# Adaptive-norm gates spread by a DMA, retention split from PSUM, decay moved behind the projection

## The chip, the cores and the metric

The kernel runs on one core of a Trainium2 chip. The metric is the device time of one execution in microseconds (us); a smaller number is better. A core has five engines with instruction streams of their own: TensorE (PE in the profile, weight loads under PEld), VectorE (DVE), ScalarE (ACT), GpSimd (POOL) and SyncE (SP), which here only issues DMA transfers. Each stream is worked off in order; the engines wait for each other through semaphores.

## What is computed

The program is a two-layer encoder on 256 tokens of width 1024. One layer of the reference, cut:

```python
cond = jax.nn.silu(c)
mod = (cond @ w_ada[i] + b_ada[i])[:, None, :]
sh1, sc1, g1, sh2, sc2, g2 = jnp.split(mod, 6, axis=-1)
h = _rmsnorm(x, norm1_g[i]) * (1.0 + sc1) + sh1
q_a, k_a, v_a, u_s, q_r, k_r, v_r, g_r = jnp.split(h @ w_in[i], split_at, axis=-1)
...                      # attention y_a, S5 scan y_s, retention y_r (each from its columns)
mixed = jnp.concatenate([y_a, y_s, y_r], axis=-1) @ w_out[i]
x = x + g1 * mixed
h = _rmsnorm(x, norm2_g[i]) * (1.0 + sc2) + sh2
x = x + g2 * _hier_moe(h, ...)
# retention, per head: scores (rotated q, k) times a decay gamma^(i-j), times v;
# then each head is normalised, scaled by gn_g and gated by silu(g_r)
```

The adaptive-norm rows of one layer are 6144 numbers. The two gates g1 and g2 multiply whole rows, so the kernel needs them repeated on all 128 partitions. The shifts and scales are needed as columns.

## The kernel before

The token axis is two blocks of 128 (t). Each layer has a mixing stage, then an expert stage.

In the mixing stage the weights of the projections come in 1 MB pieces on SP's queue. Each piece is split into a high part by ScalarE (L685) and a low part by VectorE (L686), and three products of the parts make one exact product on TensorE: `product`, whose matmuls are L710 (tokens on the partitions) and L705 (turned). The input projection runs five blocks of columns: block 0 is retention's q and k, block 1 its v and gate, blocks 2 to 4 the attention's. At the end of a block a function evicts the bank from PSUM: L845 (`to_qkr`, on VectorE, times the decay), L841, L849 and L852 (copies on ScalarE). TensorE's order is written by hand: `at(g, f)` puts a piece of other work between the steps of the projection. That is the S5 scan (matmuls L463 and L497; VectorE's products L473 to L476, the scan L480, and L483 and L484 behind it, whose result L497 needs), retention (`rope`, `turn`, `scores`, `mix`, `out`) and the remaining adaptive-norm products. The order of the other engines follows from a scheduler with priorities, in which the weight splits stand high.

The adaptive norm (`ada_slot`) has three groups of 2048 numbers per layer. The first is done ahead of the stage; groups 1 and 2 are sixteen steps within the projection, each four matmuls (L204) that leave the same row on 32 partitions. After eight steps `ada_row` copies the sum out of PSUM on ScalarE (L228), and `ada_finish` transposes it on TensorE (L234) and adds the bias on VectorE (L235), so that `modT` holds columns. `gate_row` (L243) makes a row on all partitions out of such columns: four matmuls of a repeated column with the identity (L250) and an eviction on ScalarE (L251), twice for 1024 columns. It is called for g1 among the fillers of the output projection (`fill`, between the attention's L579) and for g2 in the route of the expert stage (`filler`), ahead of the next layer's first adaptive-norm group (L204).

In retention `scores` multiplies the two diagonal blocks by a mask on VectorE (L630) and copies the third on ScalarE (L632); `mix` copies the output out of PSUM on ScalarE (L643) and normalises it on VectorE (L645 to L659); `out` transposes it on TensorE (L665), scales it out of PSUM into SBUF on VectorE (L669, one per 128 columns), rounds it on ScalarE (L672) and subtracts on VectorE (L673), which leaves the high and low part for the output projection. Behind L672 stand ScalarE's weight splits and L852.

In the expert stage the weights of 32 experts stream through rings of buffers on SP's queue, after a route that picks two experts for each token (mask `mb` on VectorE, L1010; its matmul L1013).

## Time and profile before

| | us |
|---|---|
| median of 3 runs | 878.51 (877.28 to 881.81) |
| profiled execution | 879.31 |
| its span, first to last instruction | 877.4 |
| TensorE busy | 731.9 (83%) |
| VectorE busy | 486.1 (55%) |
| ScalarE busy | 243.9 (28%) |
| GpSimd busy | 114.3 (13%) |

The mean granted TensorE clock is 0.929 of full speed. The mixing stages last from about 48 to 195 in layer 0 and 460 to 622 in layer 1; the routes lie behind them, then the expert stages. A share over the whole span says little, since the stages differ: in the expert stages DMA is busy nearly all of the time, in the mixing stages 0.5 to 0.8. The timeline rows below give the start, the duration, the engine, the line, the operation with output and inputs, shape and count, and in brackets the idle time ahead of the group with the instruction that ended it.

### The profile page before, as it was taken

The page shows a single profiled execution, that of the slowest core. Times are in us where ns is not written, and L with a number is a line of the kernel's source. Part 1 is how long each engine was busy: PE and PEld are TensorE (multiplying, and loading weights), DVE is VectorE, ACT ScalarE, POOL GpSimd, SP SyncE. Part 2 cuts the span into 40 slices and gives each one's busy share as a digit, 9 for nine tenths or more (in the row PEclk, how much of TensorE's full clock was granted, in tenths as well). Part 3 has the DMA queues.
Part 4 walks back from the last instruction along what each step waited for, and adds up shares of the span by engine and source line. Part 5 has one row for each costly group of instructions (what it writes and reads, how often), then busy time and mean ns, then how long its engine had stood idle before and what let it go on. Part 6 is the DMA issues. An engine that isn't in the chain of part 4 may idle for free. (4 is left out here: it accounts for less than half of the span.)

```text
span 877.4 us, 11506 instructions
## 1 busy us (share of the span) xinstructions
PE 731.9 (83%) x4174; PEld 397.0 (45%) x4174; DVE 486.1 (55%) x1065; ACT 243.9 (28%) x520; POOL 114.3 (13%) x163
## 2 busy tenths in 40 slices
PE   3688998989999995987688979889799999498864
PEld 0454775775535332422127558567653533242211
DVE  6789896454754354231148979955675435423114
ACT  1532435831312110210025223386231211020002
POOL 0553050001100000000025401300110000000000
PEclk9699999997999996999897989999999999699898
DMA  9976687776999789999999646669549988999992
GB/s 372 421 305 255 232 340 293 302 267 238 393 412 397 314 342 416 383 418 415 417 418 377 239 149 246 258 232 361 195 193 405 403 328 349 402 399 420 415 416 106
DMA packets 50309, 290.48 MB, mean 331 GB/s; under 512 B 4544, under 2 KB 4800, under 8 KB 24896
## 3 DMA queue, kind: packets, MB, share of 16 engines
q1 hardware_dynamic: 49536, 287.78, 82.6%
q10 hardware_dynamic: 704, 1.84, 0.5%
q8 instruction: 36, 0.59, 0.3%
q14 instruction: 33, 0.27, 0.1%
HBM read 288.55 MB, written 1.05 MB: 330 GB/s over the span
## 5 line engine op out<-in xcount | busy, mean ns | idle before, releaser
L1180 PE MATMUL mm<-ring,b 128*32 128x512 f32 (+1 forms) x584 | 116.6, 601 | 14.4 <-DMA ring<-in_wgu_dram 14.4
L686 DVE TENSOR_TENSOR wh<-w,wh 128x512 fp32r<-128x512 f32 x120 | 91.2, 776 | 35.9 <-ACT wh L685 35.3
L1180 PE MATMUL mm<-w,b 128*32 128x512 f32 (+1 forms) x440 | 98.7, 665 | 11.3 <-DMA w<-in_wgu_dram 11.3
L1186 DVE SCALAR_TENSOR_TENSOR b<-mm,cw,b 128x256 f32<-128x256 f32 x22 | 10.6, 483 | 167.9 <-ACT b L1184 167.9
L685 ACT ACTIVATE wh<-w 128x512 fp32r<-128x512 f32 x120 | 73.9, 628 | 81.3 <-PE mm L710 48.0
L710 PE MATMUL mm<-wh,early 128*128 128x512 f32 x288 | 81.7, 428 | 10.1 <-ACT b L852 6.0
L1205 PE MATMUL sc<-ring,b 128*32 128x512 f32 (+1 forms) x312 | 67.5, 616 | 7.7 <-ACT b L1194 4.0
L710 PEld LDWEIGHTS mm<-wh,early 128*128 128x128 f32 x288 | 54.4, 199 | 36.0 <-issue 8.5
L1180 PEld LDWEIGHTS mm<-ring,b 128*32 128x32 f32 (+1 forms) x584 | 31.1, 120 | 76.2 <-issue 49.1
L204 PE MATMUL ac<-w,cc 128*32 128x512 f32 x320 | 47.0, 673 | 18.4 <-DVE cc L198 11.6
L1184 ACT ACTIVATE b<-mm 128x256 f32<-128x256 f32 x22 | 8.5, 384 | 187.8 <-PE mm L1180 187.8
L1214 DVE TENSOR_TENSOR y<-sc,gr 128x512 f32<-128x512 f32 x44 | 30.4, 691 | 48.8 <-PE sc L1205 47.1
L1180 PEld LDWEIGHTS mm<-w,b 128*32 128x32 f32 (+1 forms) x440 | 25.7, 130 | 67.3 <-issue 45.3
L1219 ACT ACTIVATE y<-y 128x512 fp32r<-128x512 f32 x40 | 25.2, 630 | 94.4 <-DVE y L1214 85.3
L705 PE MATMUL mm<-early,wh 128*128 128x256 f32 x384 | 50.4, 286 | 0.0
L1205 PE MATMUL sc<-w,b 128*32 128x512 f32 (+1 forms) x200 | 46.2, 666 | 4.7 <-DMA w<-in_moe_w_down_dram 3.2
L705 PEld LDWEIGHTS mm<-early,wh 128*128 128x128 f32 x384 | 46.8, 188 | 6.0 <-issue 4.5
L1160 POOL TENSOR_TENSOR b<-b,comd 128x128 f32<-128x128 f32 x32 | 12.9, 425 | 275.9 <-DVE b L1094 118.6
L710 PE MATMUL mm<-wh,big 128*128 128x512 f32 x192 | 47.6, 398 | 1.4 <-DVE y L896 1.4
L1144 PE MATMUL tr<-b,big 128*128 128x512 f32 (+2 forms) x128 | 31.4, 387 | 20.2 <-DVE b L1094 19.8
L710 PEld LDWEIGHTS mm<-wh,big 128*128 128x128 f32 x192 | 35.0, 188 | 9.2 <-DVE y L896 2.2
L1144 PEld LDWEIGHTS tr<-b,big 128*128 128x128 f32 x128 | 23.5, 218 | 28.2 <-issue 23.2
(350 smaller groups left out, 1123.7 us busy)
## 6 DMA issues: line engine op xcount, KB each, us to landing
ring<-in_wgu_dram SPq DMA_DIRECT2D x73, 1024.0 KB, 11.1
w<-in_wgu_dram SPq DMA_DIRECT2D x55, 1024.0 KB, 10.3
w<-in_w_ada_dram SPq DMA_DIRECT2D x40, 1024.0 KB, 9.2
ring<-in_moe_w_down_dram SPq DMA_DIRECT2D x39, 1024.0 KB, 12.8
w<-in_moe_w_down_dram SPq DMA_DIRECT2D x25, 1024.0 KB, 12.3
w<-in_win_dram SPq DMA_DIRECT2D x22, 1024.0 KB, 6.9
w<-in_w_out_dram SPq DMA_DIRECT2D x8, 1024.0 KB, 7.2
ring<-in_w_ada_dram SPq DMA_DIRECT2D x8, 1024.0 KB, 10.4
```

The lines of the kernel that those rows point to most:

```text
L204: PE.matmul(acc[32 * t:32 * t + 32, :], c1[:, k:k + 1].to_broadcast([128, 32]), w[:, t * 512:(t + 1) * 512], start=(k == 0), stop=(k == 7) ...
L685: A.activation(wh[:, 0], w, AF.Copy)
L686: lo_eng[par_[0] % len(lo_eng)].tensor_tensor(wh[:, 1], w, wh[:, 0].bitcast(F32), op=ALU.subtract)
L705: PE.matmul(pt[t][:, f * 256:(f + 1) * 256], whs[i][:, w_, fs], a[x_][:, k], start=first and f + m == 0, stop=end and m == 2, skip_group_c ...
L710: PE.matmul(pt[t], a[x_][:, k, ts_], whs[i][:, w_], start=first and m == 0, stop=end and m == 2)
L1144: PE.matmul(pc[c], (xlo if i else xhi)[:, t, cs], Dm[blk][:, t, ss], start=(i + t == 0), stop=(i + t == 3))
L1160: G.tensor_tensor(Dc[:, t].rearrange("p (e s) -> p e s", s=w), Dm[blk][:, t, po:po + 128].bitcast(F32).rearrange("p (e s) -> p e s", s=w), ...
L1180: PE.matmul(gu[o:o + w, :], hg[blk, k][:, po + o:po + o + w], ws[k // 4][j][:, k % 4] if ahead else part_gu(l, es[j], k), start=(k == 0), ...
L1186: V.scalar_tensor_tensor(act, gu[:, 256:512], cw, si, op0=ALU.mult, op1=ALU.mult)
L1205: PE.matmul(yp[h][o:o + w, :], aT[:, f * 128 + o:f * 128 + o + w], wd[j][:, f, h] if ahead else part_wd(l, es[j], f, h), start=(f == 0), s ...
L1214: V.tensor_tensor(y, yp[h], gr2[:, h * 512:(h + 1) * 512], op=ALU.mult)
L1219: A.activation(yh, y, AF.Copy)
```

## The change

Four edits are made. The gates: `ada_gate` takes the place of `ada_row` for groups 1 and 2, adds a bias row on VectorE as it copies the sum out of PSUM, and issues two DMA transfers on ScalarE's queue that spread the 32-partition blocks of the gate to 128 partitions; the bias row is a new load of 256 KB, also on ScalarE's queue. `ada_biased` then only copies the columns. The 64 matmul records of `gate_row` and their eight evictions go (`along` stays for the last norm). The gate of the second half has a buffer of its own. Second, retention's output is scaled and rounded by ScalarE straight from PSUM, and VectorE computes the low part from PSUM in one operation per 128 columns. Third, the decay leaves the projection's eviction (now a ScalarE copy): the part of the key goes into the masked scores (eight operations on 128 columns for four on two blocks, and the scale of ScalarE's copy), the part of the query into `mix`, whose copy becomes a product on VectorE. Fourth, the pool b2 has 13 buffers instead of 14, and a small tensor `hgn` holds half of the norm's gain.

```diff
-        BUFS = {"mix": {"early": 3, "b2": 14, "bT": 2, "r4": 2, "big": 2, "b4": 4, "y2": 8, "b1": 6, "wh": 5,
+        BUFS = {"mix": {"early": 3, "b2": 13, "bT": 2, "r4": 2, "big": 2, "b4": 4, "y2": 8, "b1": 6, "wh": 5,
...
             if k == 0:
                 ada_acc[l, g] = ps("ac")
+                b = bias_row[l, g] = sb([128, 512], "bad")
+                A.dma_start(b, I["badar"][l, g - 1])
             acc = ada_acc[l, g]
             w = ahead.pop((l, "ada", j), None) or load_ada(l, g, k)
             ada_mm(acc, k, w)
             if k == 7:
-                ada_acc[l, g] = ada_row(acc)
+                ada_acc[l, g] = ada_gate(l, g, acc)
         def ada_row(acc):
             row = y2([128, 512])
             A.activation(row, acc, AF.Copy)
             return row
+
+        gates, bias_row = {}, {}
+
+        def ada_gate(l, g, acc):
+
+
+            row = y2([128, 512])
+            V.tensor_tensor(row, acc, bias_row.pop((l, g)), op=ALU.add)
+            gr = gates[l, g] = b4([128, 1024]) if g == 1 else cp.tile([128, 1024], F32, name=nm("gr2"), tag="gr2")
+            for h in range(2):
+                o = 32 * (2 * g - 2 + h)
+                A.dma_start(gr[:, h * 512:(h + 1) * 512], row[o:o + 32, :].unsqueeze(1).to_broadcast([32, 4, 512]))
+            return row
+
+        def ada_biased(l, g, row):
+            tp = ps("tr")
+            for f in range(4):
+                PE.transpose(tp[:, f * 128:(f + 1) * 128], row[:, f * 128:(f + 1) * 128], ident)
+            V.tensor_copy(modT[l][:, g * 16:(g + 1) * 16].rearrange("p (t f) -> p t f", t=4),
+                          tp.rearrange("p (f t r) -> p t f r", f=4, t=4)[:, :, :, 0])
         def ada_finish(l, g, row):
             tp = ps("tr")
...
             return modT[l][:, i * 8:(i + 1) * 8]
-
-        def gate_row(l, i, dst, h):
-            along(mod(l, i), dst, h)
...
             V.tensor_scalar(hb, Pm(l, "bglu"), 0.5, None, op0=ALU.mult)
-            return bt, ncim, hb
+            hg = sb([128, 2], "hgn")
+            V.tensor_scalar(hg, Pm(l, "gng"), 0.5, None, op0=ALU.mult)
+            return bt, ncim, hb, hg
...
                     s = T_["s"][2 * c + j]
-                    s3, sc3 = (a.rearrange("p (b q) -> p b q", b=3) for a in (s, sc[:, 0:384]))
-                    V.tensor_tensor(s3[:, 0:3:2], sc3[:, 0:3:2], C("tri")[:, None, :].to_broadcast([128, 2, 128]),
-                                    op=ALU.mult)
-                    A.activation(s[:, 128:256], sc[:, 128:256], AF.Copy)
+                    d = [C("decay")[:, t * 8 + 4 + 2 * c + j:][:, 0:1] for t in range(2)]
+                    for t in range(2):
+                        q = slice(256 * t, 256 * t + 128)
+                        V.scalar_tensor_tensor(s[:, q], sc[:, q], d[t], C("tri"), op0=ALU.mult, op1=ALU.mult)
+                    A.activation(s[:, 128:256], sc[:, 128:256], AF.Copy, scale=d[0])
             def mix(t):
                 sT = T_["s"]
                 y = b1_([128, 4, 64])
-                A.activation(y.rearrange("p h e -> p (h e)"), yp[:, 0:256], AF.Copy)
+                V.tensor_tensor(y, yp[:, 0:256].rearrange("p (h e) -> p h e", h=4),
+                                C("decay")[:, t * 8:t * 8 + 4].unsqueeze(2).to_broadcast([128, 4, 64]), op=ALU.mult)
                 mu = sb([128, 4], "rmu")
                 V.tensor_reduce(mu, y, axis=AX.X, op=ALU.add)
                 V.tensor_scalar(mu, mu, 1.0 / 64, None, op0=ALU.mult)
                     PE.transpose(tp[:, c * 128:(c + 1) * 128], tg[:, c * 128:(c + 1) * 128], ident)
-                gng = Pm(l, "gng")
-                yr = b1_([128, 2, 128])
+                tk = slice(t * 128, (t + 1) * 128)
                 for c in range(2):
-                    V.tensor_scalar(yr[:, c], tp[:, c * 128:(c + 1) * 128],
-                                    gng[:, c:c + 1], 0.5, op0=ALU.mult, op1=ALU.mult)
-                tk = slice(t * 128, (t + 1) * 128)
-                A.activation(yT[0][:, 6:8, tk], yr, AF.Copy)
-                V.tensor_tensor(yT[1][:, 6:8, tk], yr, yT[0][:, 6:8, tk].bitcast(F32), op=ALU.subtract)
+                    yc, gn = tp[:, c * 128:(c + 1) * 128], prep[3][:, c:c + 1]
+                    A.activation(yT[0][:, 6 + c, tk], yc, AF.Copy, scale=gn)
+                    V.scalar_tensor_tensor(yT[1][:, 6 + c, tk], yc, gn, yT[0][:, 6 + c, tk].bitcast(F32),
+                                           op0=ALU.mult, op1=ALU.subtract)
             return start, rope, turn, scores, mix, out
                     if j % 8 == 7:
-                        at(g + 1, lambda i: ada_finish(l, i, ada_acc[l, i]), 1 + j // 8)
+                        at(g + 1, lambda i: ada_biased(l, i, ada_acc[l, i]), 1 + j // 8)
                 qkr, vgr = r4
-                start, rope, rturn, rscores, rmix, rout = retention(l, qkr, vgr, yT)
+                start, rope, rturn, rscores, rmix, rout = retention(prep, qkr, vgr, yT)
                 at(7, start)
                 at(8, rope, 0)
                 at(8, rope, 1)
-                def to_qkr(t, p):
-                    d = C("decay")[:, t * 8:(t + 1) * 8].unsqueeze(2).to_broadcast([128, 8, 64])
-                    V.tensor_tensor(qkr[:, t].rearrange("p (h f) -> p h f", h=8),
-                                    p.rearrange("p (h f) -> p h f", h=8), d, op=ALU.mult)
-
                 def to_q(t, p):
                     A.activation(qT[:, 2 * t:2 * t + 2, :], p.rearrange("p (f s) -> p f s", f=2), AF.Copy, scale=0.125)
                 def to_k(t, p):
                     A.activation(kT[:, 2 * t:2 * t + 2, :], p.rearrange("p (f s) -> p f s", f=2), AF.Copy)
-                for b, (turned, evac) in enumerate(((False, to_qkr), (False, to_token(vgr)), (True, to_q), (True, to_k),
+                for b, (turned, evac) in enumerate(((False, to_token(qkr)), (False, to_token(vgr)), (True, to_q), (True, to_k),
                                                     (False, to_token(v)))):
                     product(h2, get_win(b), range(8), turned, evac, lambda i: run(8 * b + i))
                 wo = wo[2:] + wo[:2]
-                gr1 = b4([128, 1024])
+                gr1 = gates[l, 1]
...
                 fill = [(out_chunk, (k,)) for k in (6, 7, 4, 5)]
-                fill += [(gate_row, (l, 2, gr1, h)) for h in range(2)]
                 def next_fill():
...
         def moe(l, more):
-            gr2 = sb([128, 1024], "gr2")
+            gr2 = gates[l, 2]
             turn[0] = 0
             nxt = [(k, load_ada(l + 1, 0, k, wslot())) for k in range(8)] if more else []
             acc = ps("ac") if more else None
-            rows = [(l, 5, gr2, h) for h in range(2)]
-
             def filler(n):
-                if rows and n > 1:
-                    for a in rows:
-                        gate_row(*a)
-                    del rows[:]
                 for k, w in nxt[:n]:
                     ada_mm(acc, k, w)
                     if k == 7:
...
+    badar = np.repeat(inp["b_ada"].reshape(L, 3, 4, 1, 512)[:, 1:], 32, axis=3).reshape(L, 2, 128, 512)
```

On TensorE, at the end of layer 0's attention (L579 multiplies probabilities and values; `modT` are the columns, `prb` the route's weights), the order before is:

```order
L579 MATMUL ac_1665<-y_319_1600,b_97_488 64x128
L579 MATMUL ac_1665<-y_324_1617,b_97_488 64x128
L250 MATMUL tr_1672<-cst,modT_97 128x128 x4
L250 MATMUL tr_1678<-cst,modT_97 128x128 x4
L579 MATMUL ac_1684<-y_328_1639,b_97_488 64x256
L579 MATMUL ac_1684<-y_331_1654,b_97_488 64x256
L579 MATMUL ac_1684<-y_328_1639,b_97_488 64x128
L579 MATMUL ac_1684<-y_331_1654,b_97_488 64x128
L921 MATMUL tr_1693<-modT_97,prb_84 40x1 x8
```

In the changed kernel, where L600 and L936 are the lines of L579 and L921:

```order
L600 MATMUL ac_1678<-y_321_1613,b_98_490 64x128
L600 MATMUL ac_1678<-y_326_1630,b_98_490 64x128
L600 MATMUL ac_1685<-y_330_1652,b_98_490 64x256
L600 MATMUL ac_1685<-y_333_1667,b_98_490 64x256
L600 MATMUL ac_1685<-y_330_1652,b_98_490 64x128
L600 MATMUL ac_1685<-y_333_1667,b_98_490 64x128
L936 MATMUL tr_1694<-modT_97,prb_84 40x1 x8
```

The two groups of four matmuls are gone, and the two attention groups follow each other.

On VectorE, in layer 0 at retention's output (`tr` is the transposed output, `b_235` the scan's result that L497 needs, `wh` a weight split, `big` the projection's input), the order before is:

```order
L474 TENSOR_TENSOR b_236_1187<-sc_1170,b_217_1061 128x512
L669 TENSOR_SCALAR b_243_1238<-tr_1235,par_333 128x128
L475 TENSOR_TENSOR b_235_1186<-b_235_1186,b_236_1187 128x256
L476 TENSOR_TENSOR b_235_1186<-b_235_1186,b_236_1187 128x256
L669 TENSOR_SCALAR b_243_1238<-tr_1235,par_333 128x128
L480 SCALAR_TENSOR_TENSOR b_236_1187<-radius,b_235_1186 128x256 x2
L669 TENSOR_SCALAR b_247_1261<-tr_1258,par_333 128x128
L483 TENSOR_TENSOR b_237_1194<-b_236_1187,b_217_1061 128x512
L686 TENSOR_TENSOR wh_1360<-w_1318,wh_1360 128x512
L686 TENSOR_TENSOR wh_1395<-w_1318,wh_1395 128x512
L484 TENSOR_TENSOR b_235_1186<-b_236_1187,b_217_1061 128x512
```

In the changed kernel, with L497 for L476, L501 for L480, L504 and L505 for L483 and L484, L707 for L686 and L693 for the new low part:

```order
L497 TENSOR_TENSOR b_239_1199<-b_239_1199,b_240_1200 128x256
L693 SCALAR_TENSOR_TENSOR big_337<-tr_1248,hgn_486,big_336 128x128
L501 SCALAR_TENSOR_TENSOR b_240_1200<-radius,b_239_1199 128x256 x2
L693 SCALAR_TENSOR_TENSOR big_337<-tr_1248,hgn_486,big_336 128x128
L504 TENSOR_TENSOR b_241_1207<-b_240_1200,b_221_1074 128x512
L707 TENSOR_TENSOR wh_1371<-w_1329,wh_1371 128x512
L505 TENSOR_TENSOR b_239_1199<-b_240_1200,b_221_1074 128x512
L707 TENSOR_TENSOR wh_1406<-w_1329,wh_1406 128x512
```

One of the two weight splits now stands behind the scan's last operation, and the third scaling is gone from ahead of it; the scans themselves keep their places.

On ScalarE, in layer 1 ahead of the attention's exponentials (L556, and L577 in the changed kernel), the order before is:

```order
L685 ACTIVATE wh_6915<-w_6860 128x512
L228 ACTIVATE y_1811_6807<-ac_6192 128x512
L511 ACTIVATE b_1822_6847<-b_1822_6847 128x512
L556 ACT_TABLE_LOAD
L556 ACTIVATE y_1814_6815,smx_6817<-y_1814_6815,mx_6816 128x256
L685 ACTIVATE wh_7036<-w_6950 128x512
```

In the changed kernel, where L706 is the weight split L685:

```order
L706 ACTIVATE wh_6917<-w_6862 128x512
L243 DMA gr_1811_6808<-y_1810_6806 128x1x512 x2
L706 ACTIVATE wh_7037<-w_6952 128x512
L577 ACT_TABLE_LOAD
L577 ACTIVATE y_1814_6817,smx_6819<-y_1814_6817,mx_6818 128x256
L706 ACTIVATE wh_7052<-w_6952 128x512
```

The copy of the adaptive-norm sum is gone, the two spreading transfers (`gr`) stand ahead of a weight split and of the table load, and L511 (a tanh of the S5 branch) has moved behind the first exponentials.

## Rows read from the trace of the kernel before

**Rows 1.** windows: us, busy time of each engine, granted clock, DMA share, GB/s
```profile
15.00:30.00 15.00, 9.12 (x52) 1.10 (x44) 9.98 (x49) 4.73 (x13) 3.14 (x5) 0.77 1.02 420
60.00:85.00 25.00, 20.21 (x104) 11.25 (x103) 24.83 (x40) 6.15 (x12) 8.59 (x10) 1.00 0.75 286
85.00:115.00 30.00, 30.00 (x246) 22.49 (x244) 25.66 (x58) 13.45 (x26) 2.75 (x3) 1.00 0.62 228
575.00:600.00 25.00, 21.36 (x124) 15.92 (x124) 12.07 (x46) 23.25 (x73) 1.27 (x1) 1.00 0.74 299
630.00:640.00 10.00, 5.28 (x26) 4.83 (x27) 9.79 (x35) 2.68 (x7) 2.03 (x4) 0.67 0.01 2
```

**Rows 2.** timeline (start us, us, engine, line): TensorE, one ScalarE, out projection
```profile
171.39 2.05 PE L250 MATMUL tr<-cst,modT 128*128 128x128 f32 x16
173.37 0.87 PE L579 MATMUL ac<-y,b 128*64 128x256 f32 x8
600.48 2.05 PE L250 MATMUL tr<-cst,modT 128*128 128x128 f32 x16
169.51 0.48 ACT L569 ACTIVATE y<-tr 128x384 f32<-128x384 f32 x1
```

**Rows 3.** timeline of TensorE, one VectorE: route of both layers
```profile
205.35 3.76 PE L250 MATMUL tr<-cst,modT 128*128 128x128 f32 x16
209.04 5.03 PE L204 MATMUL ac<-ring,cc 128*32 128x512 f32 x40
214.00 0.19 PE L1013 MATMUL tr<-mb,tri_bf 128*128 128x32 bf16 x1
631.91 0.19 PE L1013 MATMUL tr<-mb,tri_bf 128*128 128x32 bf16 x1 [2.11 <-DVE mb L1010]
209.96 0.22 DVE L1010 TENSOR_TENSOR mb<-at,bf 128x64 bf16<-128x64 f32 x1
```

**Rows 4.** TensorE's waits, whole span: total us, times, longest
```profile
PE sc L625 <- DVE b L474: 6.3, 2, 4.2
PE mm L710 <- DVE r L845: 4.1, 4, 1.4
```

**Rows 5.** single lines: count, ns min/median/max; last row: who waited
```profile
L845 DVE TENSOR_TENSOR r<-mm,cst x4: 665/682/683, 64.2 to 492.7; 128x512 f32<-128x512 f32 x4
L630 DVE TENSOR_TENSOR y<-sc,cst x8: 398/416/426, 86.3 to 523.5; 128x256 f32<-128x256 f32 x8
L554 DVE CUSTOM_DVE_ANT_0 y<-sc,r x16: 273/285/288, 141.9 to 592.5; 128x128 f32<-128x128 f32 x16
L669 DVE TENSOR_SCALAR b<-tr,par x8: 323/344/347, 129.7 to 567.5; 128x128 f32<-128x128 f32 x8
  ACT big L672: 11.6, 4
```

**Rows 6.** timeline at retention's output, both layers; brackets hold idle and releaser
```profile
134.12 0.68 DVE L484 TENSOR_TENSOR b<-b,b 128x512 f32<-128x512 f32 x1
133.00 2.37 PE L710 MATMUL mm<-wh,early 128*128 128x512 f32 x9 [2.63 <-ACT b L852]
135.30 1.07 PE L497 MATMUL ac<-b,par 128*32 128x256 f32 x16
565.67 0.69 DVE L484 TENSOR_TENSOR b<-b,b 128x512 f32<-128x512 f32 x1
563.68 2.98 PE L710 MATMUL mm<-wh,early 128*128 128x512 f32 x9 [3.42 <-ACT b L852]
566.60 1.94 PE L497 MATMUL ac<-b,par 128*32 128x256 f32 x16
```

**Rows 7.** timeline after layer 0's last adaLN matmul: TensorE, ScalarE
```profile
147.06 0.66 PE L234 MATMUL tr<-cst,y 128*128 128x128 f32 x4 [2.33 <-ACT y L228]
149.07 0.51 ACT L556 ACTIVATE y<-y,mx 128x256 f32<-128x256 f32 x1 [1.37 <-DVE mx L552]
```

**Rows 8.** timeline of ScalarE's queue: one DMA issue at the start
```profile
1.18 0.46 ACTq L161 DMA_DIRECT2D x<-in_x_dram  x1
```

More of the change, by code (lines that the diff above doesn't have):

```diff
@@ L584, in attention, with retention @@
             return scores, turn, mix
-        def retention(l, qkr, vgr, yT):
+        def retention(prep, qkr, vgr, yT):
             cos = C("cos").rearrange("p (t f) -> p t f", t=2)
@@ L1496, in prepare @@
     return {"x": inp["x"], "cst": cst, "par": par, "prb": prb, "w_ada": inp["w_ada"], "win": win, "bias": bias,
-            "w_out": inp["w_out"], "wgu": wgu.reshape(L, NE, 2, 128, 2048), "moe_w_down": inp["moe_w_down"]}
+            "w_out": inp["w_out"], "badar": badar, "wgu": wgu.reshape(L, NE, 2, 128, 2048), "moe_w_down": inp["moe_w_down"]}
 def kernel(**inputs):
```

## The prediction, made before the changed kernel was run

> **What bounds the kernel now.** I began with the busy times by stage. The kernel alternates between two kinds of stage, and they have different limits. In the expert stages the weights stream in and TensorE waits for them, so nothing that the change touches counts there; but the stream restarts only when the route before it is done, since its buffers are full by then (from 630 to 640, in layer 1's route, DMA is busy 0.01 of the time [rows 1]), so whatever shortens the stage ahead moves the whole expert stage forward. In the mixing stages the limit moves from engine to engine: VectorE is busy 24.83 of 25 us from 60 to 85, TensorE 30.00 of 30 us from 85 to 115, and ScalarE 23.25 of 25 us during layer 1's softmax (575 to 600) [rows 1]. So an edit there is worth what it takes off the engine that is late at that point, and a stall that goes is worth only the distance to the next late engine. I read next the timeline of TensorE with the idle time before each group, and for each gap the engine that ended it.
>
> **Gate matmuls in the output projection.** In each layer sixteen matmul records (eight matmuls) take 2.05 us, and the next group starts 1.98 us after they started, in layer 0 from 171.39 to 173.37 [rows 2]. Before and after them TensorE runs without a gap, and the input of the next group, ScalarE's copy of transposed probabilities, was there at 169.99 (169.51 and 0.48) [rows 2]. Nothing else becomes late, so both layers gain 1.98: **-4.0**. Their two evictions on ScalarE go with them.
>
> **Gate matmuls in the route.** In layer 0 they take 3.76 us, because TensorE is at the lower level there, 1.2 GHz (the same sixteen take 2.05 in the projection at 2.4 GHz) [rows 2, 3]. Behind them stand 40 matmuls of the next adaLN and then the mask matmul at 214.00, whose input was ready at 210.18 (209.96 and 0.22) [rows 3]: TensorE is the late one by 3.8. If the clock rises at the same moment as before, the work removed is worth its full-clock time, 1.98; if it rises earlier relative to the work, up to 3.76. I take **-1.9**, the nearer to an unchanged clock, ends 0 and -3.8. In layer 1 there is no next adaLN; TensorE already waits 2.11 us for VectorE's mask [rows 3], and the removal only widens that gap: **0**.
>
> **Decay out of the projection's eviction.** VectorE loses two evictions of 0.682 per layer [rows 5]; ScalarE takes them as plain copies, and it is busy 6.15 of 25 us there [rows 1]. TensorE waited for these evictions 4.1 us in four places, and then 6.3 us in two places for VectorE's scan products (L474) [rows 4]. The second wait shows that VectorE is simply behind, so shortening the first wait lengthens the second unless VectorE loses work. What counts is VectorE's sum up to L474: in layer 0 it loses 1.36 and gains one operation on two columns, which I leave out. In layer 1 the order puts the first biased copy ahead of that point; it reads 512 columns from PSUM as L845 did, so 0.68 comes back. **-1.4 and -0.7**, ends 0 and -4.1 (all of the first wait).
>
> **Decay into mask and outputs.** Four products of 0.416 per layer become eight on 128 columns. No row has that form; the nearest are 0.285 and 0.344 [rows 5], so 2.3 to 2.75 in place of 1.66, and I take +0.9 (0.3 each). The biased copy of layer 0 (0.68) stands behind them. Both lie where TensorE is busy without a gap and VectorE has 30.00 less 25.66, or 4.3 us, idle [rows 1]; this cover hides them, and without it they cost 1.6 in layer 0. The two products at the outputs (128 by 256 from PSUM, as L630, 0.416) replace ScalarE copies and stand after that idle time, in a chain that ends in the saturated stretch: **0.8 per layer later** on VectorE from there, which enters the next step.
>
> **Retention's output.** Before, ScalarE waited 11.6 us in four places for VectorE's L669 [rows 5], and TensorE behind it 2.63 and 3.42 for a bank [rows 6]. After, ScalarE reads PSUM itself and need not wait for VectorE. But look at what stands next: TensorE's L497 needs the scan output of L484. In layer 0, L484 ended at 134.80 and L497 began at 135.30; the new order puts behind it one weight split (0.68, the time of L484, which has as many columns) and takes away one L669 (0.34), so with the 0.8 above it ends at 134.58, a gain of 0.7 rather than 2.63. In layer 1 the order before L484 keeps its length; it ended at 566.36, now 567.16, while L497 began at 566.60: a loss of 0.55 [rows 6]. Sum **-0.15**; ends -6.05 (both gaps wholly gone) and +1.6 (the delay of 0.8 twice, no gain).
>
> **Biased rows and the spread.** In layer 0 TensorE waited 2.33 for ScalarE's copy of the second adaLN sum, which stood behind softmax work [rows 7]. VectorE is free there, so the wait goes. ScalarE is the next late engine: it was idle 1.37 behind that same gap [rows 7], loses a copy of at most 0.68 (L845 has as many columns [rows 5]) and gains two DMA issues of 0.46 [rows 8]; this path gives 1.13. Between 1.13 and 2.33 I take **-1.7**, ends 0 and -2.33. In layer 1 the two issues stand ahead of a table load and the first exponentials, in a stretch where ScalarE sets the pace [rows 1]: **+0.9**. Queued behind them are two weight splits and all of the softmax. The other spreads lie under TensorE's work; eight issues uncovered would be 3.7. Each bias load is 0.26 MB, which at 420 GB/s [rows 1] is 0.62 us in a stretch where DMA is full; two such (one per layer) give 0 to 1.2, I take **+0.6**. The load of the parameters waits for a lane with the first of them on SP's queue; its data are needed well after it, so I count nothing. Nor do I for the buffer that b2 loses: GpSimd's table work then waits for a scan that is done long before, and GpSimd is busy 8.59 of 25 us at its fullest [rows 1]; uncovered, it would hold TensorE as VectorE's scans do now, 4.2 at worst [rows 4].
>
> **Sum.** -4.0 -1.9 -2.1 -0.15 -1.7 +0.9 +0.6 = -8.3 us. Against the profiled execution (879.3, of which the span is 877.4) this gives 871.0; that execution was 0.8 above the median of 878.5, so the median should be **870.2**.
>
> **A rule to weigh.** The same sixteen matmuls take 3.76 us at the half clock and 2.05 at the full one [rows 2, 3], and removing filler leaves TensorE idler. The Trainium skill, page "TensorE: Matmul & The Clock Gate", section "Why this matters for your kernels", advises against idle gaps between bursts, since a gap drops the array to half rate; by that rule the gate matmuls in the route were useful as filler. The trace does not decide it, since layer 0's filler ran at half clock itself. What the rule would give is the fourth rival.
>
> **The rivals.** (1) *VectorE is not next late.* If the new order lets the scans run ahead, both gaps at the output go whole (5.9 more) and so does the wait for L845 (2.0 more): 862.3. For it: ScalarE's stall really is removed. Against: the ends of L484 within 0.6 us of L497's start [rows 6]. Chance 0.20. (2) *VectorE becomes the bound.* Scores, outputs and biased copies add more than the evictions give back: no gain at the projection (+2.1), the output step at its worse end (+1.75), no gain at the adaLN gap (+1.7): 875.8. For it: saturation from 60 to 85; against: the cover of 4.3. Chance 0.15. (3) *ScalarE is held by the spread.* Its DMA issue waits in order for VectorE's biased copy, as L672 waited for L669, with weight splits and evictions behind it, in four places. At 2.9 each (11.6 over 4 [rows 5]) this costs 11.6: 881.8, **slower than before**. It passes 878.5 from 2.1 us per place and half a per cent from 3.2; at 4.2, VectorE's longest lateness [rows 4], it would be 887. Against it: in three of the four places VectorE has idle time or does the copy first. Chance 0.07. (4) *The clock stays low in the route.* The 40 matmuls then take 10.06 instead of 5.03 from 205.35 on and end at 215.4, 1.3 late instead of 1.9 early, and layer 1's wider gap costs between 0 and as much, so 3.2 and 1.6: 875.0. Chance 0.08.
>
> **How the numbers follow.** The forecast has 0.50, its own range 866 to 874.5. A measurement of this kernel can tell about 0.5% (4.4 us) from no change, so faster means under 874.1 and slower over 882.9. Faster: 0.48 of the forecast, 0.20, 0.05 of the second rival, 0.03 of the fourth, together 0.76. Slower: 0.04 of the third. Same: the rest, 0.20. The range from 861 to 876.5 leaves out the third rival, the lower part of the first and the upper tails of the second and fourth, 0.19 in all.
>
> **What would show it.** In the changed trace: TensorE's L579 groups back to back in the projection; the wait for L845 gone and the wait for L474 shorter by 1.4 and 0.7; after retention's output a TensorE wait for VectorE's scan output at L497 in place of the one for ScalarE's eviction; no wait before the transposes at 147; ScalarE's first exponential in layer 1 about a microsecond later against its neighbours; a wider gap at the mask matmul of layer 1. The forecast is wrong if ScalarE shows idle time ending in the biased copy, or if the granted clock in the route falls below what it was.

## The result and the profile after

The changed kernel took **868.25 us** (median of 4 runs, 867.36 to 869.38) and the kernel before, beside it, 878.32 (877.28 to 881.81): a ratio of 0.990, 95% interval 0.985 to 0.995. The prediction was 870.2 with a range of 861 to 876.5. The profiled execution has a span of 865.5 for 877.4, so 11.9 us went where the sum had 8.3. The number was right; most of what follows is about why its terms were not.

One thing has to be known to read the medians below. The kernel before, run 79 times beside the experiments, took from 868.4 us (granted clock 0.950 over the span) to 883.7 (0.923), and the other kernels with ten runs or more spread by 6 to 14 us. A median of 4 to 12 runs is therefore uncertain by some microseconds, and the reasons are read from traces, by one method: the start of a TensorE instruction that two kernels share, in the one less in the other. The table gives these shifts in us (negative is earlier). "Again" is a second profile of the changed kernel; the other columns are experiments below.

| at (before's time) | changed | again | b2_13 | pair_first | pair_pool | decay_alone | no_gates |
|---|---|---|---|---|---|---|---|
| 84.57 scores, layer 0 (L625) | -1.64 | -3.88 | -1.56 | -2.28 | -2.59 | -0.56 | -2.88 |
| 90.24 projection (L705) | 1.28 | -0.94 | -1.18 | 0.65 | 0.34 | 1.34 | 0.18 |
| 128.41 adaLN (L204) | 1.46 | -0.77 | -1.15 | 2.31 | 0.35 | 1.37 | 0.19 |
| 138.03 behind the scan output (L710) | 3.02 | 1.46 | 1.58 | 1.92 | -0.11 | 3.84 | 1.82 |
| 154.70 gate of S5 (L524) | -1.08 | -2.64 | 0.04 | -2.18 | -4.22 | 5.08 | 4.46 |
| 159.97 attention scores (L543) | 2.06 | 2.08 | 0.06 | 1.15 | -3.07 | 5.07 | 4.46 |
| 192.79 end of mixing (L942) | -0.01 | -0.23 | 0.08 | -1.12 | -5.18 | 5.11 | 4.50 |
| 214.00 mask, layer 0 (L1013) | -8.29 | -8.50 | -7.96 | -9.39 | -8.62 | -1.31 | -3.54 |
| 458.65 start of layer 1 (L763) | -8.45 | -8.61 | -5.67 | -9.91 | -7.88 | -3.09 | -3.11 |
| 526.23 retention, layer 1 (L639) | -13.41 | -14.23 | -9.52 | -15.33 | -14.13 | -7.56 | -8.56 |
| 603.16 end of softmax (L921) | -14.23 | -12.96 | -9.38 | -13.88 | -14.28 | -6.33 | -8.12 |

Read the first column downwards. All of layer 0's mixing stage ends with nothing gained (-0.01). The route, 22 us long, gains 8.3. Layer 1's mixing stage gains 5.8, and the last expert stage gives 2.3 back.

TensorE's timeline of the changed kernel, at the places of [rows 2], [rows 3] and [rows 6] and at three waits (start us, us, engine, line; in brackets idle time ahead and what ended it):

```profile
82.93 1.61 PE L646 MATMUL sc<-y,y 64*128 64x256 f32 x6 [2.26 <-DVE b L495]
84.47 5.25 PE L731 MATMUL mm<-wh,early 128*128 128x512 f32 x12
133.62 4.76 PE L731 MATMUL mm<-wh,early 128*128 128x512 f32 x12 [2.69 <-ACT b L868]
138.32 1.07 PE L518 MATMUL ac<-b,par 128*32 128x256 f32 x16
159.09 0.92 PE L564 MATMUL sc<-b,b 64*128 64x256 f32 x6 [2.63 <-ACT b L547]
172.69 1.52 PE L600 MATMUL ac<-y,b 128*64 128x256 f32 x16
174.04 0.74 PE L936 MATMUL tr<-modT,prb 128*40 128x1 f32 x16
201.28 4.50 PE L204 MATMUL ac<-ring,cc 128*32 128x512 f32 x40
205.71 0.19 PE L1028 MATMUL tr<-mb,tri_bf 128*128 128x32 bf16 x1
587.59 1.52 PE L600 MATMUL ac<-y,b 128*64 128x256 f32 x16
588.93 0.74 PE L936 MATMUL tr<-modT,prb 128*40 128x1 f32 x16
```

The gate matmuls are gone from the projection: the last two attention groups take 1.35 us together. Three waits of over 2.2 us stand in layer 0's mixing stage, and the work behind them is slow: the twelve matmuls at 84.47 took 5.25 us where the same twelve took 3.07 before.

Windows of the changed kernel (us, busy time of TensorE, its weight loads, VectorE, ScalarE, GpSimd; then the granted clock, DMA share, GB/s) and the same windows of the kernel before:

```profile
84.00:90.00 6.00, 6.00 (x19) 4.20 (x21) 5.93 (x13) 2.24 (x5) 0.77 (x1) 0.56 0.33 139
130.00:140.00 10.00, 7.31 (x52) 4.18 (x52) 9.11 (x18) 4.42 (x9) 0.00 (x0) 0.83 0.90 342
155.00:165.00 10.00, 7.37 (x42) 5.28 (x41) 4.44 (x21) 9.62 (x33) 1.27 (x1) 0.83 0.94 368
192.00:214.00 22.00, 18.46 (x148) 11.28 (x146) 14.81 (x53) 7.11 (x15) 5.12 (x6) 1.00 0.87 334
```

```profile
84.00:90.00 6.00, 5.43 (x32) 3.60 (x34) 5.96 (x13) 2.48 (x7) 0.00 (x0) 1.00 0.44 184
130.00:140.00 10.00, 7.37 (x61) 4.22 (x61) 9.36 (x21) 4.13 (x9) 0.00 (x0) 1.00 0.63 229
155.00:165.00 10.00, 9.08 (x58) 6.94 (x57) 5.82 (x24) 9.62 (x31) 1.28 (x1) 1.00 0.58 220
192.00:214.00 22.00, 20.13 (x118) 13.99 (x116) 8.82 (x39) 5.63 (x12) 2.29 (x2) 0.69 0.52 177
```

So the stretches at the lower level, 1.2 GHz, have moved. Before, one lay in the route; after, parts of the mixing stage lie at it, and the route runs at 2.4 GHz throughout. This trade was not in the sum. A wait alone does not bring it about: before, TensorE waited 2.63 us at 133.00 [rows 6] and 2.33 at 147.06 [rows 7], with 1.00 in the window behind the first.

TensorE's waits after (us, times, longest), with those of [rows 4] first:

```profile
PE sc L646 <- DVE b L495: 6.5, 2, 4.3
PE mm L731 <- ACT b L868: 6.5, 2, 3.8
PE sc L564 <- ACT b L547: 4.7, 2, 2.6
PE tr L1028 <- DVE mb L1025: 4.0, 1, 4.0
```

The wait for L845 (4.1) is gone, as foretold, and the mask's gap in layer 1 has grown from 2.11 to 4.0, as foretold. But the wait for the scan products (L495, before L474) did not shorten, and at retention's output TensorE still waits for ScalarE's eviction (L868, before L852). ScalarE's timeline shows why:

```profile
132.72 0.37 ACT L692 ACTIVATE big<-tr,hgn 128x128 fp32r<-128x128 f32 x1 [5.97 <-DVE big L693]
132.98 0.59 ACT L868 ACTIVATE b<-mm 128x512 f32<-128x512 f32 x1
548.30 0.37 ACT L692 ACTIVATE big<-tr,hgn 128x128 fp32r<-128x128 f32 x1 [4.82 <-DVE big L693]
550.02 0.58 ACT L868 ACTIVATE b<-mm 128x512 f32<-128x512 f32 x1
559.79 1.41 ACTq L243 DMA_DIRECT2D gr<-y  x2
563.27 0.51 ACT L577 ACTIVATE y<-y,mx 128x256 f32<-128x256 f32 x1
```

ScalarE stands 5.97 and 4.82 us in front of its second copy (L692) until VectorE has finished the low part of the first (L693). Both read the same PSUM tile `tr`, in program order copy, low part, copy, low part.

### The profile page after: what moved, and what is told of

The parts are those of the page before. It is cut to its first block, busy times and chain, and to the rows that moved or that the text cites. A ratio compares the mean times of both kernels' runs of the same rounds, so it can differ in the third digit from the quotient of the medians.

```text
span 865.5 us, 11404 instructions
## 1 busy us (share of the span) xinstructions
PE 723.1 (84%) x4110; PEld 389.5 (45%) x4110; DVE 486.2 (56%) x1075; ACT 240.4 (28%) x512; POOL 110.2 (13%) x163
## 5 line engine op out<-in xcount | busy, mean ns | idle before, releaser
L1195 PE MATMUL mm<-w,b 128*32 128x512 f32 (+1 forms) x440 | 98.7, 659 | 10.7 <-DMA w<-in_wgu_dram 10.7
L707 DVE TENSOR_TENSOR wh<-w,wh 128x512 fp32r<-128x512 f32 x120 | 89.2, 757 | 30.5 <-ACT wh L706 29.9
L706 ACT ACTIVATE wh<-w 128x512 fp32r<-128x512 f32 x120 | 74.4, 630 | 87.2 <-PE mm L731 48.3
L204 PE MATMUL ac<-w,cc 128*32 128x512 f32 x320 | 46.6, 667 | 19.3 <-DVE cc L198 11.6
```

Of the source, the lines that this page charges most:

```text
L204: PE.matmul(acc[32 * t:32 * t + 32, :], c1[:, k:k + 1].to_broadcast([128, 32]), w[:, t * 512:(t + 1) * 512], start=(k == 0), stop=(k == 7) ...
L706: A.activation(wh[:, 0], w, AF.Copy)
L707: lo_eng[par_[0] % len(lo_eng)].tensor_tensor(wh[:, 1], w, wh[:, 0].bitcast(F32), op=ALU.subtract)
L1195: PE.matmul(gu[o:o + w, :], hg[blk, k][:, po + o:po + o + w], ws[k // 4][j][:, k % 4] if ahead else part_gu(l, es[j], k), start=(k == 0), ...
```

## Experiments

**The changed kernel again.** No edit.

> The changed kernel again, on the chip of the other runs of this call. If the four runs of the first measurement were typical: 868 to 869, ratio 0.99 to before. If before's spread between chips was the cause of a part: 0.993 to 0.996.

868.66 us (866.63 to 874.83, 12 runs), before 877.43 (23 runs): 0.992, interval 0.989 to 0.996. The gain holds, at the lower end. Its profile ends layer 0's mixing at -0.23 and gains 8.3 in the route again, so the pattern of the first column is no accident of one execution. The kernel before was profiled only once, in an execution of 879.31. Of its 79 runs, 17 took less than 871 us, at clocks of 0.936 to 0.950; how their routes ran is not known.

**ScalarE's copies first.**

```diff
-    for c in range(2): copy(c) on ScalarE; low part(c) on VectorE
+    for c in range(2): copy(c) on ScalarE
+    for c in range(2): low part(c) on VectorE
```

> The changed kernel (868.3), with retention's two rounding copies on ScalarE written ahead of the two low parts on VectorE. Theory: ScalarE's second copy waits (5.97 and 4.82 us) because VectorE's low part of the first half reads the same PSUM bank in between, and TensorE waits behind it (2.69 and 3.80). Then both waits go; TensorE next waits for the scan output, which ended at 135.91 and 553.37, so L518 comes 2.4 earlier in layer 0 and 0.9 in layer 1: 865.0. Rival A, VectorE was never next late: both gaps go whole, 6.5 less, 861.8. Rival B, the eviction waits for something else: no change, 868.3.

867.87 us (10 runs), 0.991 (0.987 to 0.995): the time of rival B, but not its reason. ScalarE's wait went, and TensorE's wait for L868 with it. What took its place:

```profile
PE ac L518 <- DVE b L504: 2.9, 2, 2.7
PE ac L518 <- DVE b L505: 1.7, 2, 1.2
135.88 0.64 PE L518 MATMUL ac<-b,par 128*32 128x256 f32 x8 [0.16 <-DVE b L504]
137.68 0.40 PE L518 MATMUL ac<-b,par 128*32 128x256 f32 x1 [1.17 <-DVE b L505]
```

TensorE now waits at L518 for VectorE's scan output. From 128.41 to 138.03 it gains 0.39 where the changed kernel lost 1.56, so 1.95 for a gap of 2.69, near the 2.4 of the theory; in layer 1 (559.32 to 572.00) it loses 0.41 where the changed kernel lost 0.09. The window from 130 to 140 ran at 1.00 in the three kernels with the copies first, and at 0.66 to 0.83 in all others but before. The logic of the prediction's output term (VectorE is next late there) is shown; its premise, that ScalarE need not wait for VectorE, held only with the copies first.

**The bias load later**, and both together.

```diff
-    if k == 0: load the bias row      # ahead of the group's eight steps
+    if k == 5: load the bias row
```

> The changed kernel with the load of the bias row issued at the sixth of the eight adaptive-norm steps instead of the first. Theory: the first load of layer 0 stands in a stretch where DMA is full and holds the parameter load on SP's queue (issued at 20.82 instead of 17.18), which cost 1.35 us up to 49 us; moved out of that stretch it gives 1.1 to 1.35 back, and 0 to 0.6 in layer 1: 866.8. Rival: the start is late for another reason (the added bytes alone, or the order of the weight loads): 868.3.

869.04 us (10 runs), 0.992 (0.988 to 0.997): nothing. The first load still issues at the same time, since nothing on its queue holds it back, so the experiment hardly moved it. In the changed kernel TensorE stands 1.34 us late at 61.34 in one profile and 0.88 early in the other, in bias_late 0.51 late: executions of one kernel differ there by more than the load could cost, so its price is not resolved.

> Both repairs together on the changed kernel: the copies first and the bias load late. If both theories hold and add, 3.3 and 1.4 less than 868.3: 863.6. If only one holds, 865 or 866.8.

865.62 us (862.3 to 870.1, 4 runs), 0.987 (0.980 to 0.995). With four runs this is not distinguished from pair_first.

**Each edit taken back from the changed kernel.**

```diff
 # no_gates: rows by repeated columns and the identity, as before
-    ada_gate, ada_biased, two spreading transfers
+    ada_row, ada_finish, gate_row in the projection and in the route
 # no_out: retention's output by L669, L672, L673 as before
 # no_decay: decay in the projection's eviction as before
```

> The changed kernel with the gate edit undone (gates by matmuls again, no bias rows, no spread); retention's two edits stay. Theory that the clock in layer 0's route stayed high by its phase and not through the removal: the gates are worth 4.2 in the projections, 2 to 3.8 in the route and 1 at the adaptive norm, less 1.35 at the start, so 875 to 876, and the granted clock in the route may be either level. Rival, the removal itself keeps the clock high: the route alone is worth 7.8, so 879.5 to 880, with the clock at half from 196 on as before.

> The changed kernel with the output edit undone (scaling on VectorE into SBUF, copy on ScalarE, subtraction on VectorE). Theory: the edit replaced one ScalarE wait for VectorE by another of the same size (11.6 us before, 7.7 and about 5 after), so it is worth nothing: 868 to 868.6. By the prediction's worse end it cost 1.6, so undone 866.7; by its better end it gave 6: 874.

> The changed kernel with the decay edit undone (decay in the projection's eviction on VectorE, mask product and output copy as before); gates and output edit stay. By the prediction's step it is worth 2.1: 870.4. By the changed trace, where TensorE stands 2.3 earlier at retention's scores in layer 0 and 3.9 in layer 1: 872.5 to 874.5. If VectorE's added operations eat it later on: 868.3.

no_gates 874.23 (10 runs, 0.999, 0.995 to 1.003), no_out 871.29 (0.996, 0.993 to 0.999), no_decay 871.87 (0.997, 0.993 to 1.001). Read as single prices these would be 6.0, 3.0 and 3.6 us, more than the changed kernel gained in all; they do not add. The traces say why for two of them. In no_gates TensorE waits for the copy L228 again, longer than before [rows 7], and it stands 4.46 us late at 154.70:

```profile
150.09 1.12 PE L254 MATMUL tr<-cst,y 128*128 128x128 f32 x4 [3.55 <-ACT y L228]
```

no_out comes out of the route 7.28 earlier and has kept 3.05 at 458.65; from 225 to 235 its granted clock was 0.66, where the changed kernel had 1.00. Its median fits none of the three expected. In no_gates the route ran at 2.4 GHz with the gate matmuls back (1.00 from 196 to 206), as its theory had it and against its rival.

**The decay alone on the kernel before.**

```diff
-    to_qkr: eviction times decay on VectorE;  mask only;  copy in mix
+    plain copy on ScalarE;  mask times decay per block;  product in mix
```

> The kernel before (878.3) with the decay edit alone. By the prediction 2.1 less, 876.2; by the changed trace up to 6 less, 872; if the shorter waits only lengthen later ones, 878.3. The wait for the projection's eviction of retention's q and k (4.1 us in four places) is gone in each case.

876.38 us (10 runs) beside 875.65 for before, 1.003 (0.999 to 1.007): no gain. By 68.25 the missing wait gave 2.27, of which 0.74 was left at the scores (61.34 to 84.57); the next wait had grown. In layer 0 it is 5.11 later by 192.79; from 474.12 to 526.23 in layer 1 it gains 3.0.

**The route's matmuls put back** into the changed kernel, their result unused.

```diff
     def filler(n):
+        if n > 1, once: two groups of four matmuls, repeated column of modT with the identity
```

> The changed kernel with the sixteen gate matmuls put back in both routes as filler, their result unused and not evicted; all else as changed. Theory (phase): they cost their own 1.98 at full clock in layer 0 and nothing in layer 1, with the route's clock high as in the changed kernel: 870.2. Rival, removing them is what kept the clock high: the route falls to half clock from 196 on and layer 0 loses 7.8: 876.

874.25 us (10 runs), 0.999 (0.996 to 1.002). On its trace the matmuls cost what the prediction had taken, and no more:

```profile
202.71 2.03 PE L1321 MATMUL tr<-cst,modT 128*128 128x128 f32 x16
204.68 4.50 PE L204 MATMUL ac<-ring,cc 128*32 128x512 f32 x40
```

1.97 us at 2.4 GHz. From 192.79 to 214.00 this kernel gains 6.42 with the filler in place, the changed one 8.28, so the removal is worth 1.9. Most of the route's gain has nothing to do with it. That the median rose by 6 us is not explained by these 2 us and stays open.

**One buffer fewer, alone.** The last question was the number that the prediction had counted at nothing.

```diff
-        BUFS = {"mix": {"early": 3, "b2": 14, ...
+        BUFS = {"mix": {"early": 3, "b2": 13, ...
```

> The kernel before with one number changed: the pool b2 has 13 buffers for 14. The order on every engine stays the same; GpSimd's last table step of each layer must then wait for an earlier scan's buffer. The prediction counted this at nothing. Theory: GpSimd's tables, which ran from 72 to 76 beside VectorE in the stretch where VectorE sets the pace, move to about 82 to 85, and TensorE stands about 1.5 us earlier at retention's scores of layer 0 (before-time 84.6) and 1 to 3 us earlier in layer 1; time 874 to 876 beside 877 to 878 of before. Rival: the buffer is worth nothing, the shift at 84.6 stays within 0.5 us and the time within 1 us of before.

**866.7 us** (864.3 to 869.7, 4 runs), before 877.43: 0.988, interval 0.982 to 0.995. No instruction differs from the kernel before or stands elsewhere in any engine's order, and the time is that of the whole change, well below the 874 to 876 of the theory. The trace of the kernel before, VectorE and GpSimd in layer 0:

```profile
72.24 1.21 DVE L603 TENSOR_TENSOR y<-r,cst 128x512 f32<-128x512 f32 x1
73.38 0.84 DVE L604 TENSOR_TENSOR y<-r,cst 128x256 f32<-128x256 f32 x1
74.14 3.45 DVE L686 TENSOR_TENSOR wh<-w,wh 128x512 fp32r<-128x512 f32 x4
74.78 1.06 POOL L455 TENSOR_TENSOR b<-b,b 128x256 f32<-128x256 f32 x1
```

and of b2_13 (VectorE, GpSimd, and TensorE's wait at the scores):

```profile
72.61 0.68 DVE L603 TENSOR_TENSOR y<-r,cst 128x512 f32<-128x512 f32 x1
73.21 0.41 DVE L604 TENSOR_TENSOR y<-r,cst 128x256 f32<-128x256 f32 x1
73.54 2.48 DVE L686 TENSOR_TENSOR wh<-w,wh 128x512 fp32r<-128x512 f32 x4
82.19 0.68 DVE L474 TENSOR_TENSOR b<-sc,b 128x512 f32<-128x512 f32 x1
81.81 0.73 POOL L452 TENSOR_TENSOR b<-b,b 128x256 f32<-128x256 f32 x1 [9.41 <-DVE b L484]
83.01 0.89 PE L625 MATMUL sc<-y,y 64*128 64x256 f32 x6 [1.03 <-DVE b L474]
```

Before, GpSimd wrote its last scan tables (L450 to L455) up to 75.84, beside VectorE's rope and weight splits; L603 then takes 1.21 us for 0.68, L604 0.84 for 0.41, four splits 3.45 for 2.48: 1.9 us in all. With 13 buffers the last four table operations wait 9.41 us for a scan to release a buffer and run at 81.8, beside L474, which reads PSUM and takes 0.68 there as anywhere. VectorE, 0.37 late before this stretch, reaches the scan products 1.56 earlier, and TensorE's scores follow by as much. The Trainium skill, page "SBUF — State Buffer", section "Who interferes with whom", states that a VectorE instruction with two SBUF inputs contends with a GpSimd instruction that reads SBUF, and one with at most one SBUF input, outside the two-port modes, does not. The traces agree: L603 and L604 have two SBUF inputs, L474 has one of its two in PSUM.

That gives 1.9 up to layer 0's scores, of which nothing is left at the end of the mixing stage (+0.08; from 130 to 140 the clock was 0.66), and 3.2 in layer 1 (from 474.12 to 526.23, -6.33 to -9.52). Most of b2_13's gain is in the route, -8.0, where the level was 2.4 GHz, with the filler in place:

```profile
196.00:206.00 10.00, 10.00 (x89) 5.79 (x88) 5.94 (x31) 3.45 (x7) 2.25 (x2) 1.00 0.96 357
199.65 2.03 PE L250 MATMUL tr<-cst,modT 128*128 128x128 f32 x16
```

It came to the route at the same time as before (+0.08) and left it 8 us earlier. In no_decay, which has no filler, the same window was at 0.53, as in the kernel before:

```profile
196.00:206.00 10.00, 10.00 (x53) 6.85 (x56) 2.77 (x13) 2.48 (x5) 1.57 (x1) 0.53 0.70 261
```

So neither the presence nor the absence of the gate matmuls decides the level there: from 196 to 206 one of the six traces with them lies below 1.00 (before), and two of the eight without (no_decay and, at 0.66, pair_pool). What does is open: b2_13 had only 0.25 us of idle time ahead of this stretch where before had 1.87, but the changed kernel had 1.88 and ran at 2.4 GHz.

**The decay with 13 buffers.** decay_alone with the edit above.

> The decay edit alone on the kernel before (as in decay_alone), now with b2 at 13. Theory that the buffer adds to the decay: TensorE at before-time 84.6 stands 2 us earlier than before (decay_alone: 0.56 earlier), and the 4.1 us that decay_alone lost between 496.8 and 509 in layer 1 shrink to about 1; time 872 to 874. Rival: as decay_alone, 876.4.

874.57 us (10 runs, one of them of 3696.8 us; the other nine have 874.12), 0.997 (0.993 to 1.001), nearer the theory's 872 to 874 than the rival. Scores at 84.57 stand 2.49 earlier, for 0.56 without the buffer, and the 4.1 us lost in layer 1 shrink to 0.6. But the edits share their gain in layer 1: from 474.12 to 526.23 the decay alone gives 3.0, the buffer alone 3.2, both 3.9. And it leaves the route 3.76 early but starts layer 1 only 0.29 early, for the lower level came next in the expert stage, where the changed kernel had 1.00:

```profile
225.00:235.00 10.00, 9.48 (x54) 6.30 (x52) 7.56 (x13) 2.59 (x6) 0.76 (x2) 0.82 1.01 402
235.00:245.00 10.00, 10.00 (x42) 3.00 (x40) 0.61 (x2) 0.38 (x1) 0.00 (x0) 0.84 0.60 223
```

**The spread on GpSimd's queue**, with ScalarE's copies first.

```diff
-    A.dma_start(gr[...], row[...])     # ScalarE's queue
+    G.dma_start(gr[...], row[...])     # GpSimd's queue
```

> The changed kernel with both ScalarE copies of retention's output ahead of both of VectorE's low parts (as in pair_first), and the spreading transfers issued on GpSimd's queue for ScalarE's. Theory: ScalarE's issues of 1.24 to 1.41 us per pair stand in its softmax stretch and are what the softmax gave back; without them layer 1's exponentials begin about 1.4 us earlier and layer 0's up to 1.4, time 865 to 866.5 (pair_first: 867.9). Rival: GpSimd's issue waits for VectorE's biased copy with scan tables queued behind it, and takes its own time: TensorE's wait for VectorE's scan products grows in layer 1, 868 to 871.

**865.63 us** (863.52 to 866.95, 6 runs), 0.988 (0.983 to 0.993), 3.0 below the changed kernel beside it. The scheduler also reorders ScalarE's softmax around the missing issues. In layer 0:

```profile
144.09 1.18 POOL L243 DMA_DIRECT2D gr<-y  x2 [17.30 <-DVE y L239]
154.45 0.92 PE L564 MATMUL sc<-b,b 64*128 64x256 f32 x6 [1.12 <-ACT b L547]
196.00:206.00 10.00, 10.00 (x63) 4.90 (x66) 5.08 (x28) 0.42 (x2) 0.00 (x0) 0.66 0.69 231
```

The wait for ScalarE at L564 falls from 2.63 to 1.12, and the mixing stage ends 5.18 early, for 1.12 in pair_first. About half of these 4 us was there at 128.41 (0.35 for 2.31), and that half is not the issues' doing: 24 matmuls, ahead of the first pair in both kernels (97.61 in pair_first), ran slowly in pair_first and not here (first line pair_first, second pair_pool):

```profile
90.89 4.63 PE L727 MATMUL mm<-early,wh 128*128 128x256 f32 x24
90.58 3.13 PE L727 MATMUL mm<-early,wh 128*128 128x256 f32 x24
```

The other 2 us come behind the second pair, between 154.70 and 159.97. The issues on ScalarE, with the order that the scheduler made around them, cost at most that. Then the route falls to 0.66 of the clock and keeps 3.4 of the 8.3 that the others gain there. In layer 1 the softmax stretch (577.14 to 599.68) loses 0.8 for 3.2 in pair_first; but the changed kernel's own two profiles have 1.2 and 3.1 there, so the theory's 1.4 is not shown. The median is the theory's, and the lowest of the kernels with more than four runs, though it is not shown to beat b2_13 (866.7, 4 runs).

## Why the prediction was right, and where it was right by luck

Each term against the shifts of the changed kernel:

- **Out-projection, -4.0: right.** From the last attention pair to L921 it took 3.48 us before (170.59 to 174.07) and 1.35 after; layer 1 reads the same to 0.01 (587.59 to 588.93): -4.3.
- **Route, -1.9 and 0: right in mechanism.** The filler is worth 1.97 at full clock; layer 1 gains nothing (-14.23 before its route, -14.21 behind the mask). Set beside route_filler, the removal gave the 1.9 of the sum. What the sum did not have is 6.4 us more in layer 0. The prediction chose "an unchanged clock" and gave the other end 3.8. The end was too near: it priced only the removed matmuls at the other level, not the route itself, which runs at 1.2 GHz in one kernel and at 2.4 in the next. Rival 4 had the right concern, that the level changes, with the sign reversed; its cause, the lost filler, is not borne out: without filler the changed kernel ran at 1.00 there and no_decay at 0.53, with it b2_13 at 1.00 and before at 0.53.
- **b2, counted at nothing: wrong.** "GpSimd's table work then waits for a scan that is done long before" was false: it waits 9.41 us, and this wait takes its work away from VectorE's, worth 1.9 up to layer 0's scores and 3.2 in layer 1 when made alone. The step looked at whether the wait delays TensorE and not at what GpSimd's work does to VectorE beside it.
- **Decay out of the eviction, -1.4 and -0.7: right in the step, half the size in layer 0.** The wait for L845 went and the next wait grew, as said. From 61.34 to 84.57 the changed kernel gained 2.98 and no_decay, with the same buffers, 2.24; the edit alone gave 0.74 too. From 474.12 to 526.23 in layer 1 the changed kernel gained 3.7 (-9.71 to -13.41) and no_decay 2.8, so 0.9 beside the buffer, though 3.0 alone. In layer 0 2.9 were lost by 90.24, most of it in the slow matmuls at 84.47.
- **Decay into mask and outputs, +0.9 hidden and +0.8: size confirmed in part.** The new products take 0.34 us each for the 0.3 assumed. The +0.8 cannot be separated from the next item.
- **Retention's output, -0.15: wrong in the step, worse in the result.** The failed step is "ScalarE reads PSUM itself and need not wait for VectorE". The wait for the eviction stayed (2.69 for 2.63 in layer 0). TensorE loses 1.6 there (128.41 to 138.03), for the twelve matmuls behind it ran in 4.76 us, partly at 1.2 GHz (clock 0.83 from 130 to 140); b2_13, with the output as before, lost 2.7 there at 0.66, so this loss is not the edit's alone. In layer 1 0.1 was lost for the 0.55 of the sum. A row before had shown the pattern and was not read: L632, ScalarE's copy of the third score block, waited in all 8.8 us, four times, for VectorE's L630 on the same bank.
- **Biased rows, -1.7: right in the step, with a later bill.** The gap at 147 is gone, and 4.1 were gained from 143 to 154.70; at 159.97 3.1 were paid back, in the wait for ScalarE's L547, so 1.0 is left. ScalarE was next late, as said; two issues cost 1.18 to 1.41 us for the 0.92 assumed. Layer 1's softmax, +0.9: it lost 1.2 in one profile and 3.1 in the other (577.14 to 599.68).
- **Bias loads, +0.6: not resolved** (1.34 late at 61.34 in one profile, 0.88 early in the other).

By stage, the shares of the sum and what the trace shows: layer 0's mixing -5.5 and 0.0, its route -1.9 and -8.3, layer 1's mixing -0.9 and -5.8, the expert stages 0 and +2.1. Layer 0's mixing gained nothing because stretches behind waits ran at the lower level and the softmax took back what the gap gave; the route's level and the buffer in layer 1 made up for it. **The total came out because errors of +7.6 and -11.3 cancelled down to -3.7.** Rival 1 (VectorE not next late) is refuted at the output by pair_first. Rival 2 (VectorE becomes the bound) is not borne out: the loss at the output, as large as its price there, lies in the clock. Rival 3 (ScalarE held by the spread) shows in one place of the changed trace:

```profile
94.76 0.63 ACT L706 ACTIVATE wh<-w 128x512 fp32r<-128x512 f32 x1 [0.55 <-PE mm L726]
96.75 1.29 ACTq L243 DMA_DIRECT2D b<-y  x2
96.03 0.69 DVE L239 TENSOR_TENSOR y<-ac,bad 128x512 f32<-128x512 f32 x1
```

ScalarE was free at 95.39 and issued when VectorE's biased copy had ended, 1.4 us later, which the prediction had named as a sign against itself. It cost nothing: ScalarE's next split began after 2.89 us of idle time, and the same split has the same 2.89 in pair_pool, where GpSimd issues.

What stays open: whether the three main edits are worth anything beyond the buffer. The changed kernel (868.3 and 868.7, 16 runs) and b2_13 (866.7, 4 runs) are not told apart, and by the traces layer 0's mixing gains nothing in either. Nor are the 10.7 us of b2_13 the price of a buffer: no_gates, route_filler and decay_b2_13 have 13 buffers too and took 874.2 to 874.6, and 8.0 of the 9.7 us by which b2_13's span is shorter come in the route, whose level is unexplained.

## What to carry to other kernels

A buffer count is a schedule: before counting a smaller pool at nothing, look up what the writer of that pool runs beside, and whether both engines read SBUF there. Moving a reader to PSUM takes one dependency away and adds another if a second engine reads the same bank, so order all reads of one engine ahead of the other's. And put the clock of each stage beside the sum: a gain of 2 us ahead of a stretch whose level can change is smaller than that change, in either sign.

## What the runs showed of the hardware

- VectorE's SBUF operations beside GpSimd's table work took up to twice their time: 0.84 for 0.41 us (128x256, two inputs in SBUF), 1.21 for 0.68 (128x512, the same); operations that read PSUM kept their 0.68.
- The same route of 22 us ran at a granted clock of 0.69 or 1.00 from nearly the same start (+0.08), which is worth 8 us; the lower level turned up elsewhere instead (from 84 to 90, 130 to 140 and 155 to 165 in the changed kernel, 225 to 245 in decay_b2_13).
- A spreading DMA of 256 KB issued on ScalarE held it for 0.55 to 0.80 us each, where a plain issue at the start took 0.46 [rows 8] and the bias rows' loads 0.33 to 1.09.
